# A fourth block evicted by VectorE straight from PSUM, and the weight and key sums moved from GpSimd to VectorE

## The chip, the cores and the metric

The kernel runs on one core of a Trainium2 chip. The metric is the device time of one launch in microseconds (us), lower is better. The core has a matrix engine (TensorE, in the profile PE, with its weight loads as PEld), VectorE (DVE), ScalarE (ACT), GpSimd (POOL), and queues for transfers between HBM and the on-chip memory SBUF, most of them issued by SyncE (SP). Matrix products are written to PSUM banks, from which another engine has to read ("evict") them before the bank is used for something else.

## The reference

One layer of a sequence model over 2048 tokens of width 1024, with 256 context tokens ahead of them. A normalised and modulated input is multiplied by one wide weight matrix `w_in` of 9216 columns. The first 5120 columns belong to eight heads of a gated linear recurrence, which runs over the tokens in both directions and starts from the states that the context leaves; the others to a gated short convolution. Both results, side by side, go through one output matrix.

```python
h  = rmsnorm(x, norm_w) * (1.0 + scale) + shift        # tokens
hc = rmsnorm(ctx, norm_w) * (1.0 + scale_c) + shift_c  # context
p  = h  @ w_in                                         # (2048, 9216)
pc = hc @ w_in[:, :HG_COLS]
...
f = lb + (1.0 - lb) * sigmoid(z)       # forget gates, one set per direction; keys are 1 - f
S_t = diag(f_t) S_{t-1} + k_t v_t^T;  o_t = S_t^T q_t  # both directions
y_hg = head_rmsnorm(o_f + o_b) * silu(gate)
y_cv = bg * conv3(cg * hh, conv_w) * silu(gate_cv)     # columns 5120..9215
x = x + gate_out * (concat([y_hg, y_cv]) @ w_out)
out = rmsnorm(x, final_norm_w)
```

## The kernel before

**Stages.** The profiled execution shows four: the setup (0 to about 235 us: modulation, normalisation and transposition of the tokens, first weights), the heads (to about 1450 us: eight heads, each over four groups of 512 tokens), the convolutions (to about 1985 us: blocks of 128 channels, two groups of tokens at a time) and the output projection.

**Seven products.** Every product of a 2x2 block arrangement is computed by `seven` with seven block products in place of eight, from sums of weight blocks (A11, A12, A22 and S1 to S4) and sums of token blocks (B11, B21, B22 and T1 to T4). Each block product `prod` is done in 16 bits with a high and a low part of both operands, so a block product is three matmuls for each of `nk` slices (lines 839, 840, 841 of the profile). A `seven` unit uses three PSUM banks: `a` (tile `sa`), `b` (`sb`) and `c_` (`sc`). Bank `a` takes A11B11, then S2T2, then S3T3, and last, after the next unit's first product, A22T4 (`finish`); `b` takes S1T1 and then S4B22; `c_` takes A12B21. Between these products values are evicted: `keep` lets ScalarE copy a bank to SBUF with a scale (line 846: p1, p5, u2, u3), and `plus` is one VectorE instruction that reads a bank, scales it and adds a kept tile (line 850). Of the four result blocks, the first and the second are evicted with `plus`; the third is left in bank `a` for a caller's instruction; the fourth (`c22`) is u3 + p5.

**Weights.** `load_pair` brings two blocks of 128 columns of `w_in` into a ring of three stage tiles (`ws_p`), measures their size on ScalarE (line 341) and prepares the left operands in steps that are taken one at a time between products of the unit before: `begin` finds the scale (lines 139 to 147; its last product waits for `rb_p`, line 345) and forms s1 (`s_p`, line 356); `whole` splits A11 and A12 into high (line 151, ScalarE) and low parts (line 152, VectorE), and forms A11 - A21 (line 367); then S1 is split, `sum_a` (line 373) forms S2, A22 and S2 are split, `sum_b` (line 376) forms S4, S3 and S4 are split. The tiles of the low parts are `wloa_p`, `wlob_p` and the lower half of `e_p`. The transfer of a later pair (line 333) waits until a stage tile is no longer read.

**Heads.** A unit gives two blocks of columns for one group: gates `f`, queries `q`, values `vT`, output gates `z`. Keys K and queries Q go through a tree of VectorE products with running decays (lines 414 and 421), and PE needs Q and K at each level (lines 554, 568, 578). `query_end` forms Q from q and f (line 496) and the key sum `ks` of both directions (line 498); `out_gates` multiplies the gate z with its sigmoid (line 713) and stores it.

**What sets the order.** The program is written as lists of steps with weights from a table (`PACE`), which are merged into the products by place; a scheduler then fixes the order of instructions on each engine before launch, and each engine runs its own list strictly in that order, waiting where an operand is not ready. So a moved instruction changes the neighbours of others too.

Of the kernel before, what the change touches and what calls it, by code (L numbers as in the profile page):

```python
# [50 lines left out]
def paced(weight, fn):  # L51
    """A step with its share of the time of its list of steps."""
    return PACE.get(weight, weight), fn
# [7 lines left out]
def hybrid_layer(ctx: ExitStack, tc, x, cx, w_ada, b_ada, w_in, w_out, fnorm_w, small_d, masks, ident_d, sel_d, out):  # L61
# [92 lines left out]
    # ---------------------------------------------------------------- modulation  # L154
# [53 lines left out]
    def norm_group(ntile, src, row0, m, nm, first_ops=None, space=q_tile):  # L208
# [84 lines left out]
        def combine(k, a, b, whole):  # L293
# [13 lines left out]
            if whole:  # L307
                store("B22", k, b22, G, G)
# [9 lines left out]
    # ---------------------------------------------------------------- weights  # L318
# [8 lines left out]
    def load_pair(col0, col1, nm, own=False, a21_at=None):  # L327
        """Two blocks of columns of w_in as left operands of the seven-product scheme."""
# [18 lines left out]
        def begin():  # L347
# [8 lines left out]
            G.tensor_tensor(t["s1"], a21, a22, ALU.add)  # L356
# [8 lines left out]
        def whole():  # L365
            split(w.st, stage[0], t["a"][0], t["a"][1])
            G.tensor_tensor(a21, a11, a21, ALU.subtract)
# [4 lines left out]
        def sum_a():  # L372
            G.tensor_tensor(a11, t["s1"], a11, ALU.subtract)  # L373

        def sum_b():
            G.tensor_tensor(a12, a12, a11, ALU.subtract)
# [5 lines left out]
    # ---------------------------------------------------------------- parameters of the heads  # L382
# [22 lines left out]
    # ---------------------------------------------------------------- recurrent heads  # L405
# [30 lines left out]
    class Seg:  # L436
        """Forget gates, keys, values and queries of one head over one stretch of tokens."""
# [55 lines left out]
        def query_end(s):  # L493
# [4 lines left out]
            G.tensor_tensor(s.ks, s.K[:, :s.n], s.K[:, s.n:], ALU.add)  # L498
# [207 lines left out]
    def out_gates(h1, h2, g, w):  # L706
# [3 lines left out]
        def end(i, h_):  # L710
            r = ring(f"zs{h_.hd}_{g}")
            S.activation(r, z[i], AF.Sigmoid)
            G.tensor_tensor(r, z[i], r, ALU.mult)
# [33 lines left out]
    # ---------------------------------------------------------------- convolution  # L747
    class Conv:
        """One block of channels over the two halves of tokens of one or two groups."""
# [80 lines left out]
    def seven(left, right, nk, n, nm, tick, sx, tmp, done, c11, c12, c21, c22):  # L830
        """Two by two blocks of a product in seven block products."""
# [33 lines left out]
        u3 = keep(a, "u3")  # L865
        c22(lambda dst: G.tensor_tensor(dst, u3, p5, ALU.add))  # L866
# [18 lines left out]
    # ---------------------------------------------------------------- output weights  # L885
# [10 lines left out]
    def load_C(pool, tp, names):  # L896
        """Right operands of the convolutions for the halves of two groups of tokens."""
# [40 lines left out]
    def wo_steps(k):  # L938
        """Operands of the output weights for the seven-product scheme, kept in DRAM."""
# [585 lines left out]
```

## Time and profile before

| what | value |
|---|---|
| time, three runs | 2316.42, 2318.95, 2320.67 us; median 2318.95 us |
| span of the profiled execution | 2317.1 us (its own time is this span; none other is recorded) |
| PE busy | 2140.4 us, 92% of the span |
| PE weight loads | 1478.3 us |
| VectorE busy | 1627.5 us, 70%, 3173 instructions |
| ScalarE busy | 1216.5 us, 53%, 2435 instructions |
| GpSimd busy | 551.4 us, 24%, 549 instructions |
| mean granted TensorE clock | 0.98 in the heads and the convolutions, 0.91 in the setup |

A busy PE is not a PE at full speed: matmuls are pipelined, and in short stretches the granted clock is 0.50. The shares are averages over four stages. Where an instruction is given with an idle time and a releaser, the idle time is that of its engine just before it, and the releaser is what ended the wait.

### The profile page before, as it was taken

To read this page: it belongs to the slowest core of one execution; us is meant where nothing else is said; L and a number is where in the kernel's file an instruction comes from. 1 tells how busy PE (TensorE), PEld (TensorE's weight loads), DVE (VectorE), ACT (ScalarE), POOL (GpSimd) and SP (SyncE) were. 2 spreads that over 40 slices of the span, in tenths; PEclk is the share of its full clock that TensorE was granted. 3 is DMA by queue.
4 is the path that set the end of the run, shared out by engine and by line. 5 is a ranking of instruction groups with operands and counts; after the bars stand their busy time and mean duration, and the time that the engine had idled before them with its cause. 6 is when DMAs were issued, how large, how long until landed. Compare 5 with 4: busy or idle time off the path is not lost.

```text
span 2317.1 us, 52341 instructions
## 1 busy us (share of the span) xinstructions
PE 2140.4 (92%) x21563; PEld 1478.3 (64%) x21563; DVE 1627.5 (70%) x3173; ACT 1216.5 (53%) x2435; POOL 551.4 (24%) x549
## 2 busy tenths in 40 slices
PE   4778799899998999999999999999999999999998
PEld 1667688787886887887878878444344434444443
DVE  6986866777668667777676685586677556677775
ACT  5665656565566565656765754453454333333332
POOL 2433412413124124133241231221122112000001
PEclk8889899999999999999999999999999999999999
DMA  8664333323341343234432538733332132734231
GB/s 308 210 211 166 94 125 100 141 84 106 102 149 68 104 145 105 99 101 147 153 112 91 191 126 276 234 116 105 110 125 102 60 125 74 276 101 145 91 118 55
DMA packets 191044, 309.92 MB, mean 134 GB/s; under 512 B 13138, under 2 KB 123090, under 8 KB 189012
## 3 DMA queue, kind: packets, MB, share of 16 engines
q1 hardware_dynamic: 188644, 302.64, 39.2%
q8 instruction: 169, 2.77, 0.5%
q10 hardware_dynamic: 2160, 3.93, 0.5%
q14 instruction: 71, 0.58, 0.1%
HBM read 241.50 MB, written 65.01 MB: 132 GB/s over the span
## 4 chain that ended last, share of the span: by engine, by line
PE 28%; issue 12%; DVE 6%; ACT 4%; DMA 3%; POOL 1%; SPq 0%; POOLq 0%; ACTq 0%; DVEq 0%
PE sa L839 4%; PE sa L841 4%; PE sa L840 4%; DMA ws_p<-in_w_in 2%; PE sb L839 2%; PE sb L841 2%; PE sb L840 2%; DVE wlob_p L152 1%; DVE e_p L152 1%; PE sc L839 1%; PE sc L840 1%; PE sc L841 1%; PE A L554 1%; DMA wos_a<-in_w_out 1%; ACT whia_p L151 1%
## 5 line engine op out<-in xcount | busy, mean ns | idle before, releaser
L846 ACT ACTIVATE u<-sa,sx_w 128x256 f32<-128x256 f32 (+1 forms) x228 | 118.8, 521 | 180.2 <-PE sa L841 162.9
L840 PEld LDWEIGHTS <-e_p 128*128 128x128 f16 x1368 | 135.3, 99 | 87.9 <-issue 40.0
L414 DVE TENSOR_TENSOR K<-K,tot 128x512 f32<-128x512 f32 x192 | 142.5, 742 | 69.5 <-PE A L578 27.1
L421 DVE TENSOR_TENSOR Q<-Q,tot 128x512 f32<-128x512 f32 x192 | 144.4, 752 | 56.7 <-PE A L554 56.4
L839 PEld LDWEIGHTS <-e_p 128*128 128x128 f16 x1368 | 135.1, 99 | 60.8 <-issue 5.5
L841 PEld LDWEIGHTS <-e_p 128*128 128x128 f16 x1368 | 135.4, 99 | 55.2 <-issue 4.4
L537 ACT ACTIVATE km<-K 128x512 f32<-128x512 f32 x160 | 108.9, 685 | 111.3 <-DVE K L414 81.8
L840 PEld LDWEIGHTS <-whib_p 128*128 128x128 f16 x912 | 90.1, 99 | 51.9 <-issue 17.7
L840 PEld LDWEIGHTS <-whia_p 128*128 128x128 f16 x912 | 89.6, 98 | 44.8 <-issue 13.2
L586 POOL COPY A<-Ac 32x128 f32<-32x128 f32 x128 | 67.3, 525 | 209.6 <-ACT A L582 193.4
L839 PEld LDWEIGHTS <-whib_p 128*128 128x128 f16 x912 | 90.0, 99 | 41.7 <-issue 2.8
L839 PEld LDWEIGHTS <-whia_p 128*128 128x128 f16 x912 | 89.7, 98 | 37.0 <-issue 1.2
L841 PEld LDWEIGHTS <-wlob_p 128*128 128x128 f16 x912 | 90.2, 99 | 35.6 <-issue 0.3
L841 PEld LDWEIGHTS <-wloa_p 128*128 128x128 f16 x912 | 89.6, 98 | 35.8 <-issue 1.6
L151 ACT ACTIVATE e_p<-ws_p,sc_p 128x512 f16<-128x512 f32 x108 | 77.2, 718 | 65.5 <-POOL ws_p L373 33.9
L152 DVE SCALAR_TENSOR_TENSOR e_p<-ws_p,sc_p,e_p 128x512 f16<-128x512 f32 x108 | 107.3, 1032 | 0.2 <-ACT e_p L151 0.2
L373 POOL TENSOR_TENSOR ws_p<-s_p,ws_p 128x512 f32<-128x512 f32 x36 | 56.3, 1564 | 205.2 <-DVE wloa_p L152 175.9
L341 ACT ACTIVATE junk<-ws_p 128x1024 f16<-128x1024 f32 x72 | 75.8, 1053 | 47.9 <-DMA ws_p<-in_w_in 47.6
L554 PE MATMUL A<-Q,km 128*32 128x32 f32 x5120 | 77.5, 203 | 23.9 <-DVE Q L421 21.0
L554 PEld LDWEIGHTS A<-Q,km 128*32 128x32 f32 x5120 | 58.6, 113 | 59.0 <-issue 26.9
L866 POOL TENSOR_TENSOR z<-u,p 128x256 f32<-128x256 f32 (+1 forms) x34 | 35.1, 1034 | 231.7 <-ACT u L846 227.3
L866 POOL TENSOR_TENSOR f<-u,p 128x256 f32<-128x256 f32 x31 | 27.5, 887 | 241.7 <-ACT u L846 241.7
(866 smaller groups left out, 7274.7 us busy)
## 6 DMA issues: line engine op xcount, KB each, us to landing
ws_p<-in_w_in SPq DMA_DIRECT2D x72, 512.0 KB, 4.1
y_o<-yT SPq DMA_DIRECT2D x32, 512.0 KB, 3.7
wa<-in_w_ada SPq DMA_DIRECT2D x16, 512.0 KB, 4.7
Gd<-zs SPq DMA_DIRECT2D x32, 256.0 KB, 3.2
sg<-Gd SPq DMA_DIRECT2D x32, 256.0 KB, 4.0
yT<-y SPq DMA_DIRECT2D x32, 256.0 KB, 2.3
wos_a<-in_w_out SPq DMA_DIRECT2D x16, 512.0 KB, 4.9
yT<-sg SPq DMA_DIRECT2D x64, 128.0 KB, 2.2
```

Of the source, the lines that this page charges most:

```text
L151: S.activation(hi, src, AF.Copy, scale=st[:, 0:1])
L152: V.scalar_tensor_tensor(lo, src, st[:, 0:1], hi, ALU.mult, ALU.subtract)
L341: S.activation(junk.rearrange("p (k n) -> p k n", k=KT), stage[i], AF.Abs, accum_out=r)
L414: V.tensor_tensor(m, m, sub(cur, nb + 1, [[2, np_], [-(nb + 1), 2], [0, B]]), ALU.mult)
L421: V.tensor_tensor(m, m, sub(cur, 1, [[2, np_], [nb - 1, 2], [0, B]]), ALU.mult)
L537: S.activation(sub(s.km, 0, [[2 * B, n // (2 * B)], [B, 2], [1, B]]), mix(s.K, n, B, n // (2 * B)), AF.Copy)
L554: PE.matmul(pt[j * SB:(j + 1) * SB, ch * SB:(ch + 1) * SB], s.km[:, o:o + SB], mix(s.qf, n, B, SB // (2 * B), o), start=True, stop=True)
L586: G.tensor_copy(A3[js, :, js], s.Ac[js])
L839: PE.matmul(ps, hi[:, k], rh, start=start and k == 0, stop=False, skip_group_check=not start)
L840: PE.matmul(ps, hi[:, k], right(name, 1, k), start=False, stop=False, skip_group_check=not start)
L841: PE.matmul(ps, lo[:, k], rh, start=False, stop=k == nk - 1, skip_group_check=not start)
L846: S.activation(r, ps, AF.Copy, scale=sx)
```

## The change

Seven places change engine. In `load_pair` the four weight sums (lines 356, 367, 373, 376) go from GpSimd to VectorE, and so do the key sum (line 498), the product of the output gate (line 713) and the low part of operand B22 in the setup (line 266, called from 308). In `seven`, the fourth block is no longer made of a ScalarE copy u3 and a GpSimd sum u3 + p5; one VectorE instruction reads bank `a`, scales and adds p5. In numbers of instructions: VectorE 342 more (12 + 4x36 + 32 + 32 + 122), ScalarE 122 fewer, GpSimd 554 to 212. The products are the same on PE, and so are the transfers. From line 866 on the changed file is one line shorter.

```diff
@@ combine (token operands)
             if whole:
-                store("B22", k, b22, G, G)
+                store("B22", k, b22, G)
@@ load_pair, begin
-            G.tensor_tensor(t["s1"], a21, a22, ALU.add)
+            V.tensor_tensor(t["s1"], a21, a22, ALU.add)
@@ load_pair, whole
             split(w.st, stage[0], t["a"][0], t["a"][1])
-            G.tensor_tensor(a21, a11, a21, ALU.subtract)
+            V.tensor_tensor(a21, a11, a21, ALU.subtract)
@@ load_pair, sum_a and sum_b
-            G.tensor_tensor(a11, t["s1"], a11, ALU.subtract)
+            V.tensor_tensor(a11, t["s1"], a11, ALU.subtract)
...
-            G.tensor_tensor(a12, a12, a11, ALU.subtract)
+            V.tensor_tensor(a12, a12, a11, ALU.subtract)
@@ Seg.query_end
-            G.tensor_tensor(s.ks, s.K[:, :s.n], s.K[:, s.n:], ALU.add)
+            V.tensor_tensor(s.ks, s.K[:, :s.n], s.K[:, s.n:], ALU.add)
@@ out_gates, end
             S.activation(r, z[i], AF.Sigmoid)
-            G.tensor_tensor(r, z[i], r, ALU.mult)
+            V.tensor_tensor(r, z[i], r, ALU.mult)
@@ seven
         prod(a, "S3", "T3", start=False)
-        u3 = keep(a, "u3")
-        c22(lambda dst: G.tensor_tensor(dst, u3, p5, ALU.add))
+        c22(plus(a, p5))
         prod(b, "S4", "B22", start=False)
         c12(plus(b, u2))
```

The order changes around the moved instructions. The first place is VectorE's list in the heads where the weights of a later unit are prepared while the tree of keys and queries runs (in the profiled execution from 712 us on). Before, the names being `wlob_p` and `e_p` for low parts, `ws_p` and `s_p` for weights in 32 bits, K and Q for the tree, `vT` for a block of values:

```order
L152 SCALAR_TENSOR_TENSOR wlob_p_10160<-s_p_10162,sc_p_10153,whib_p_10159 128x512
L152 SCALAR_TENSOR_TENSOR wlob_p_10160<-ws_p_10093,sc_p_10153,whib_p_10159 128x512
L414 TENSOR_TENSOR K_1_9349<-K_1_9349,tot_1_9866 128x8x2x32
L421 TENSOR_TENSOR Q_1_9843<-Q_1_9843,tot_1_9866 128x8x2x32
L152 SCALAR_TENSOR_TENSOR e_p_10161<-ws_p_10091,sc_p_10153,e_p_10161 128x512
L152 SCALAR_TENSOR_TENSOR e_p_10161<-ws_p_10093,sc_p_10153,e_p_10161 128x512
L152 SCALAR_TENSOR_TENSOR e_p_10161<-ws_p_10091,sc_p_10153,e_p_10161 128x512
L850 SCALAR_TENSOR_TENSOR vT_0_10037<-sb_10097,sx_w_8460,u_52_10170 128x256
```

The same place on VectorE after the change:

```order
L152 SCALAR_TENSOR_TENSOR wlob_p_10088<-s_p_10090,sc_p_10081,whib_p_10087 128x512
L373 TENSOR_TENSOR ws_p_10019<-s_p_10090,ws_p_10019 128x512
L152 SCALAR_TENSOR_TENSOR wlob_p_10088<-ws_p_10021,sc_p_10081,whib_p_10087 128x512
L414 TENSOR_TENSOR K_1_9283<-K_1_9283,tot_1_9796 128x8x2x32
L421 TENSOR_TENSOR Q_1_9773<-Q_1_9773,tot_1_9796 128x8x2x32
L152 SCALAR_TENSOR_TENSOR e_p_10089<-ws_p_10019,sc_p_10081,e_p_10089 128x512
L376 TENSOR_TENSOR ws_p_10019<-ws_p_10019 128x512
L152 SCALAR_TENSOR_TENSOR e_p_10089<-ws_p_10021,sc_p_10081,e_p_10089 128x512
L850 SCALAR_TENSOR_TENSOR q_0_9966<-sa_9967,sx_w_8402,p_52_10040 128x256
L152 SCALAR_TENSOR_TENSOR e_p_10089<-ws_p_10019,sc_p_10081,e_p_10089 128x512
L850 SCALAR_TENSOR_TENSOR vT_0_9965<-sb_10025,sx_w_8402,u_52_10098 128x256
```

Sum L373 now stands ahead of Q, and sum L376 and the eviction of q, the fourth block, stand between Q and vT.

The second place is PE's list at that point, the end of unit 52 and the beginning of unit 53. Before, the tile `sa_52` is bank `a` of unit 52 (its A22T4), `sa_53` that of unit 53, and A5 is a level of the tree that reads Q:

```order
L841 MATMUL sa_53_10251<-hop15B11_9341,wloa_p34_5845 128x256
L839 LDWEIGHTS whib_p11_8008
L839 MATMUL sa_52_10039<-hop15T4_9783,whib_p11_8008 128x256
L840 LDWEIGHTS whib_p11_8008
L840 MATMUL sa_52_10039<-hop15T4_9783,whib_p11_8008 128x256
L841 LDWEIGHTS wlob_p11_8009
L841 MATMUL sa_52_10039<-hop15T4_9783,wlob_p11_8009 128x256
L578 MATMUL A5_3_1_10193<-Q_3_1_9843,K_3_1_9349 64x64 x8
```

The same place on PE after the change:

```order
L841 MATMUL sa_53_10177<-hop15B11_9275,wloa_p34_5809 128x256
L578 MATMUL A5_3_1_10121<-Q_3_1_9773,K_3_1_9283 64x64 x8
L839 LDWEIGHTS e_p34_5812
L839 MATMUL sa_53_10177<-hop15T2_9554,e_p34_5812 128x256
L840 LDWEIGHTS e_p34_5812
L840 MATMUL sa_53_10177<-hop15T2_9554,e_p34_5812 128x256
```

and, at the end of the twelve matmuls of `sa_53` with `e_p34` (S2T2 of unit 53):

```order
L841 LDWEIGHTS e_p34_5812
L841 MATMUL sa_53_10177<-hop15T2_9554,e_p34_5812 128x256
L839 LDWEIGHTS whib_p11_7954
L839 MATMUL sa_52_9967<-hop15T4_9715,whib_p11_7954 128x256
L840 LDWEIGHTS whib_p11_7954
L840 MATMUL sa_52_9967<-hop15T4_9715,whib_p11_7954 128x256
```

A22T4 of unit 52 no longer starts ahead of the product with Q: that product comes first, then the twelve matmuls of S2T2 of unit 53, and A22T4 of unit 52 behind them.

The third place is VectorE's list in a block of the convolutions. Before:

```order
L152 SCALAR_TENSOR_TENSOR wloa_p_22571<-ws_p_22516,sc_p_22566,whia_p_22570 128x1024
L152 SCALAR_TENSOR_TENSOR wlob_p_22573<-s_p_22575,sc_p_22566,whib_p_22572 128x512
L152 SCALAR_TENSOR_TENSOR wlob_p_22573<-ws_p_22518,sc_p_22566,whib_p_22572 128x512
L850 SCALAR_TENSOR_TENSOR b_2_2_22600<-sc_22579,sx_w_22214,p_121_22520 128x512
L152 SCALAR_TENSOR_TENSOR e_p_22574<-ws_p_22516,sc_p_22566,e_p_22574 128x512
L799 TENSOR_TENSOR cv_2_2_22512<-b_2_2_22600,cv_2_2_22512 128x512
L152 SCALAR_TENSOR_TENSOR wpT_2_22612<-wo_2_22389,sc_wo,wpT_2_22612 128x512
L152 SCALAR_TENSOR_TENSOR e_p_22574<-ws_p_22518,sc_p_22566,e_p_22574 128x512
L152 SCALAR_TENSOR_TENSOR e_p_22574<-ws_p_22516,sc_p_22566,e_p_22574 128x512
L826 TENSOR_TENSOR sg_2_2_22630<-z_2_2_22628,sg_2_2_22630 128x512
L850 SCALAR_TENSOR_TENSOR b_2_2_22645<-sb_22522,sx_w_22214,u_121_22577 128x512
```

The same place after the change, `z` being a fourth block there and `b` a second one:

```order
L152 SCALAR_TENSOR_TENSOR wloa_p_22385<-ws_p_22330,sc_p_22380,whia_p_22384 128x1024
L152 SCALAR_TENSOR_TENSOR wlob_p_22387<-s_p_22389,sc_p_22380,whib_p_22386 128x512
L373 TENSOR_TENSOR ws_p_22330<-s_p_22389,ws_p_22330 128x512
L152 SCALAR_TENSOR_TENSOR wlob_p_22387<-ws_p_22332,sc_p_22380,whib_p_22386 128x512
L850 SCALAR_TENSOR_TENSOR b_2_2_22414<-sc_22393,sx_w_22032,p_121_22334 128x512
L152 SCALAR_TENSOR_TENSOR e_p_22388<-ws_p_22330,sc_p_22380,e_p_22388 128x512
L799 TENSOR_TENSOR cv_2_2_22326<-b_2_2_22414,cv_2_2_22326 128x512
L376 TENSOR_TENSOR ws_p_22330<-ws_p_22330 128x512
L152 SCALAR_TENSOR_TENSOR wpT_2_22426<-wo_2_22205,sc_wo,wpT_2_22426 128x512
L152 SCALAR_TENSOR_TENSOR e_p_22388<-ws_p_22332,sc_p_22380,e_p_22388 128x512
L152 SCALAR_TENSOR_TENSOR e_p_22388<-ws_p_22330,sc_p_22380,e_p_22388 128x512
L850 SCALAR_TENSOR_TENSOR z_2_2_22440<-sa_22296,sx_w_22032,p_121_22356 128x512
```

Both sums now stand among the splits, and the eviction of z stands behind the last split, ahead of the eviction of b from `sb`.

## The prediction

> **What bounds the kernel now.** I read the page's busy line first, then the four stages by their windows, then what PE waits for, then single bursts in the timeline. The window columns are busy time of PE, PEld, DVE, ACT and POOL (with counts of instructions), granted clock, share of DMA time, GB/s.
>
> ```profile
> PE 2140.4 (92%) x21563; PEld 1478.3 (64%) x21563; DVE 1627.5 (70%) x3173; ACT 1216.5 (53%) x2435; POOL 551.4 (24%) x549
> ```
>
> ```profile
> 0.00:235.00 235.00, 167.99 (x1824) 124.45 (x1825) 180.76 (x430) 139.13 (x267) 81.52 (x115) 0.91 0.65 221
> 235.00:1450.00 1215.00, 1142.66 (x15912) 981.31 (x15912) 869.62 (x1786) 736.73 (x1651) 332.07 (x341) 0.98 0.38 125
> 1450.00:1985.00 535.00, 508.84 (x2340) 227.32 (x2338) 346.86 (x516) 227.39 (x355) 116.81 (x81) 0.98 0.37 123
> 1985.00:2317.10 332.10, 320.94 (x1489) 145.26 (x1489) 230.23 (x445) 113.29 (x166) 21.01 (x13) 0.99 0.37 121
> ```
>
> PE bounds three of the four stages: it is busy for 94% to 97% of each. So nothing that VectorE, ScalarE or GpSimd do is worth more than what PE is not busy (1215.0 - 1142.7 = 72 us in the heads, 26 in the convolutions, 11 in the output) plus what it loses at a clock below 1.00 (2% of 1215 and of 535 is 24 and 11 us). The time in which PE stands is named by the waits, in us, with their number and the longest:
>
> ```profile
> PE A L554 <- DVE Q L421: 21.0, 15, 4.7
> PE sa L839 <- ACT p L846: 20.5, 10, 3.9
> PE A L578 <- DVE Q L421: 13.4, 7, 2.0
> PE sa L839 <- ACT u L846: 11.5, 10, 5.1
> PE sb L839 <- DVE vT L850: 9.3, 7, 1.7
> ```
>
> Three of the five end on VectorE, at Q and at vT. Seven waits of up to 2.0 and seven of up to 1.7 us point to something that comes once for each turn of the heads. One such turn is this:
>
> ```profile
> 712.18 0.74 DVE L152 SCALAR_TENSOR_TENSOR wlob_p<-s_p,sc_p,whib_p 128x512 f16<-128x512 f32 x1
> 712.41 1.65 POOL L373 TENSOR_TENSOR ws_p<-s_p,ws_p 128x512 f32<-128x512 f32 x1 [7.87 <-DVE wloa_p L152]
> 712.85 1.76 DVE L152 SCALAR_TENSOR_TENSOR wlob_p<-ws_p,sc_p,whib_p 128x512 f16<-128x512 f32 x1
> 714.13 1.59 POOL L376 TENSOR_TENSOR ws_p<-ws_p 128x512 f32<-128x512 f32 x1
> 714.52 1.75 DVE L414 TENSOR_TENSOR K<-K,tot 128x512 f32<-128x512 f32 x1
> ...
> 714.94 0.27 PE L839 MATMUL sa<-hop15T,whib_p 128*128 128x256 f16 x1
> ...
> 715.69 1.17 POOL L866 TENSOR_TENSOR q<-u,p 128x256 f32<-128x256 f32 x1
> 716.20 1.21 DVE L421 TENSOR_TENSOR Q<-Q,tot 128x512 f32<-128x512 f32 x1
> 716.82 1.72 POOL L498 TENSOR_TENSOR ks<-K 128x512 f32<-128x512 f32 x1
> 717.33 3.15 DVE L152 SCALAR_TENSOR_TENSOR e_p<-ws_p,sc_p,e_p 128x512 f16<-128x512 f32 x3
> 717.46 0.69 PE L578 MATMUL A<-Q,K 128*64 128x64 f32 x16 [2.03 <-DVE Q L421]
> ...
> 720.40 0.47 DVE L850 SCALAR_TENSOR_TENSOR vT<-sb,sx_w,u 128x256 f32<-128x256 f32 x1
> 720.79 0.71 DVE L414 TENSOR_TENSOR K<-K,tot 128x512 f32<-128x512 f32 x1
> 720.93 0.27 PE L839 MATMUL sb<-hop15T,whib_p 128*128 128x256 f16 x1 [1.69 <-DVE vT L850]
> 721.42 0.68 DVE L421 TENSOR_TENSOR Q<-Q,tot 128x512 f32<-128x512 f32 x1
> ```
>
> VectorE works without a gap from 712.18 to 721, and PE stands for 2.03 us at Q and for 1.69 at vT. The same instruction has two durations here: the low part `wlob_p` took 0.74 when it had begun before L373, and 1.76 when L373 had begun before it; K 1.75 behind the start of L376 and 0.71 with no GpSimd sum beside it; Q 1.21 and 0.68. What makes VectorE late is the GpSimd work beside it, which costs it about 1.0 us for each sum of 128x512.
>
> **The change part by part.** Prices come from these rows (busy time, mean ns of one, idle time ahead):
>
> ```profile
> L373 POOL TENSOR_TENSOR ws_p<-s_p,ws_p 128x512 f32<-128x512 f32 x36 | 56.3, 1564 | 205.2 <-DVE wloa_p L152 175.9 <-issue 22.8 <-PE sc L841 6.3
> L498 POOL TENSOR_TENSOR ks<-K 128x512 f32<-128x512 f32 x32 | 45.5, 1421 | 0.0
> L1426 DVE TENSOR_TENSOR x_o<-x_o,r_o 128x512 f32<-128x512 f32 x32 | 22.0, 687 | 0.4
> L850 DVE SCALAR_TENSOR_TENSOR f<-sb,sx_w,u 128x256 f32<-128x256 f32 x31 | 14.8, 478 | 18.7 <-PE sb L841 18.7
> L846 ACT ACTIVATE u<-sa,sx_w 128x256 f32<-128x256 f32 (+1 forms) x228 | 118.8, 521 | 180.2 <-PE sa L841 162.9
> ```
>
> *Added work.* A 128x512 sum on VectorE with no GpSimd beside it takes 0.69 us (L1426), an eviction of 128x256 with a sum 0.48 (L850; by the burst's rows about 0.74 for 512 columns would be the price of any such pass). 4x36 weight sums, 32 key sums and 32 gate products make 208 x 0.69 = 143 us; the 122 evictions at 0.48 to 0.74 are 59 to 90, taken as 70 since most are of 256 columns; the 12 low parts 12 x 0.48 = 6. VectorE gets about 219 us more.
>
> *Removed work.* ScalarE loses 122 x 0.52 = 64 us, GpSimd 342 instructions of 0.9 to 1.6 us. ScalarE's share is worth little, since the waits that end on ScalarE are put down to p and the other u, which stay; p is taken up below. For VectorE, the rows of the burst give 1.02 lost by `wlob_p`, 1.04 by K, 0.53 by Q and 3.15 - (3 x 0.74 - 0.14) = 1.07 by the three `e_p` (0.07 being what neighbours overlap): 3.7 us beside four moved instructions, 0.9 each. At 330 instructions, of which perhaps half run while VectorE has work (its 70%), that is 150 us. VectorE would stand some 70 us higher, at 73%, and no closer to being the bound; what counts is where in the bursts it is late.
>
> *The burst of the heads, in the order after.* The list is now wlob, L373, wlob, K, Q: 0.74 + 0.69 + 0.74 + 0.71 + 0.68 - 4 x 0.07 = 3.28, so Q ends at 715.46 in place of 717.41, and the wait of 2.03 at L578 shrinks to about 0.1. Then e, L376, e, q, e, vT: 3 x 0.74 + 0.69 + 2 x 0.47 - 5 x 0.07 = 3.50, and vT ends at 718.96, not 720.87. Ahead of A22T4 PE now has L578 (0.69) and S2T2, twelve matmuls that start 0.11 us after each other, 1.3 us. It would reach A22T4 at 717.5, where before it began at 714.94 with bank `a` long free. The bank is now freed by q on VectorE, at 715.46 + 0.74 + 0.69 + 0.74 + 0.47 - 4 x 0.07 = 717.8: 0.3 us late. A22T4 lasts until 719.1, when vT is done. PE begins the product behind vT at 719.1, against 720.93, and has S2T2 behind it, another 1.3: a gain of 3.1 against 3.72 stood. I take 2.7 for each of the seven, since the work behind may wait elsewhere: **-19 us** (between 0 and -22.7, the two rows of waits).
>
> *The waits at L554.* These come in the third burst of a turn:
>
> ```profile
> 751.75 0.65 PE L554 MATMUL A<-Q,km 128*32 128x32 f32 x32 [2.34 <-DVE Q L421]
> ...
> 744.00:751.00 7.00, 4.31 (x64) 3.29 (x63) 6.94 (x10) 4.43 (x7) 5.11 (x4) 0.99 0.38 115
> 751.00:757.80 6.80, 6.05 (x87) 4.27 (x88) 5.51 (x10) 5.01 (x8) 1.27 (x2) 0.50 0.41 144
> ```
>
> VectorE is busy 6.94 of 7.00 us there and GpSimd 5.11. After, Q stands ahead of the splits, but other levels stand behind them. I take a third of the 21.0: **-7 us** (0 to -21).
>
> *Late fourth blocks.* Every A22T4 now waits for VectorE in place of ScalarE. Away from the bursts VectorE has idle time and a 0.48 eviction is done as a 0.52 copy was; nothing. In the bursts the eviction stands behind splits. There are three bursts a turn, 24 in all; seven have the gain above, 0.3 late being in it. For the other 17 I take 0.3 each: **+5 us** (0 to +49: at worst 717.8 - 714.94 = 2.9 us each, if PE has nothing to do ahead of it).
>
> *Key sum, gate product.* Both are VectorE work of 0.69 behind the instructions that PE waits for (ks behind Q's first product, the gate product before a store). The two gate products stand on VectorE right behind z and wait for a sigmoid on ScalarE; what is queued behind them is a later Q. 32 of 0.69 with 0.5 of waiting would be +16 if PE waited for each; I take 0, since PE has a unit's products ahead of that Q; the work that covers it is those products, and where they are gone it costs the 0.69.
>
> *The convolutions.* PE waits for p, which stands behind a size measurement on ScalarE, which waits for a transfer:
>
> ```profile
> 1630.98 1.76 DVE L152 SCALAR_TENSOR_TENSOR wlob_p<-s_p,sc_p,whib_p 128x512 f16<-128x512 f32 x1
> 1632.67 1.75 DVE L152 SCALAR_TENSOR_TENSOR wlob_p<-ws_p,sc_p,whib_p 128x512 f16<-128x512 f32 x1
> ...
> 1635.00 3.07 DVE L152 SCALAR_TENSOR_TENSOR e_p<-ws_p,sc_p,e_p 128x512 f16<-128x512 f32 x3
> ...
> 1639.37 0.56 SPq L333 DMA_DIRECT2D ws_p<-in_w_in  x1
> ...
> 1644.55 1.06 ACT L341 ACTIVATE junk<-ws_p 128x1024 f16<-128x1024 f32 x1 [1.49 <-DMA ws_p<-in_w_in]
> ...
> 1646.93 0.58 PE L839 MATMUL sa<-C0T,e_p 128*128 128x512 f16 x1 [3.87 <-ACT p L846]
> ```
>
> The transfer's tile is freed when the splits end, at 1638.1. After the change the two `wlob_p` and three `e_p` lose 1.02 + 1.01 + 0.99 = 3.0 us, and L373, L376 and the z or u eviction add 0.69 + 0.69 + 0.74 - 0.21 = 1.9: the transfer is issued 1.1 us earlier, if SP's list has nothing of its own ahead. With half of it in the other kind of block, 0.8 us for each of eight, of the 2.6 that 20.5 / 8 makes: **-6 us** (+8 to -20: above nothing, if the eviction of z ahead of b holds PE by 0.9 a block).
>
> *Clock.* The two windows above show 0.50 in a stretch in which PE was busy 6.05 of 6.80, behind one in which it stood for 2.7 of 7.00. The clock costs at most 24 + 11 us in the two stages; if a sixth of these stretches goes with the waits, **-5 us** (0 to -35). [...]
>
> *Setup and output.* In the setup VectorE is busy 180.76 of 235.00, about as much as PE; its 12 low parts and first weight sums add what the slowing takes off: 0 (-8 to +8, 12 of 0.7 either way). In the output GpSimd has 21.0 us and PE 320.94 of 332.10: 0. The low part's cover is ScalarE's next operand, and if that is gone it costs 0.48 each, which is in the 8.
>
> Sum: -19 - 7 + 5 - 6 - 5 = -32. From the span 2317.1 that is 2285; the median of the three runs stands 1.85 above the span, so I forecast **2286 us**.
>
> **The rivals.**
>
> *A, slower: the fourth block's eviction holds PE.* ScalarE did the u3 copy at once (idle ahead of it at `sa` L841 162.9 us, so it is an engine that waits for PE); VectorE in a burst is busy 6.94 of 7.00. If in the 17 other bursts A22T4 has nothing ahead of it, each loses up to 2.9, +49 and not +5, and the third of L554 is lost too: -19 + 49 - 6 + 0 = +24, **2343 us**. It decides when the average lateness in those 17 passes 1.5 us (17 x 1.5 = 25, the gain of the first burst and of the convolutions). For it: the q eviction stands behind L376 and two splits. Against it: in the burst PE's list has S2T2 ahead of A22T4.
>
> *B, the same: nothing is won in the bursts.* The added 0.69 eats up the 0.9 of slowing removed, PE's waits go from Q and vT to the next thing, and the convolutions stay at the transfer (1.49 us of waiting at L341). Then only the +5 and a few us of clock stand: **2316 to 2321 us**. Against it: in the burst four moved instructions give 3.7 and cost 0.69 x 2 + 0.47, because ks comes later. [...]
>
> *C, more: the clock stays up.* If most waits in the bursts go below what takes the clock to 0.50, 24 of the 35 us come on top of -32: **2261 us**. The window 744 to 751 shows that it takes only 2.7 us of standing, so that most would have to vanish.
>
> *D: VectorE is slow in the bursts for another reason* (ScalarE's splits, transfers); then the moved sums are only added: 7 x (0.69 + 1.85) + 8 x 1.9 = +33, **2352 us**. Against it: K and Q took 0.71 and 0.68 at 720.79 and 721.42, in the same burst.
>
> **How the numbers follow.** Main case 0.54 (its own range 2270 to 2304), C 0.12, B 0.14, A 0.16, D 0.04. The range reaches from C to a mild A: 2258 to 2332, leaving out about half of A and D and the ends of C, 0.18. Runs of this kernel lie 0.2% apart (2316.42 to 2320.67), so 0.2%, 4.6 us, is what can be told from no change. Faster: the main case, C and 0.03 of B, 0.69; same: 0.09 of B and 0.02 of A, 0.11; slower: 0.14 of A, D and 0.02 of B, 0.20.
>
> **What would show it.** Right: VectorE's `wlob_p` and `e_p` at 0.74 all through the bursts; L578's wait for Q below 3 us in all; vT's wait below 4; VectorE busy near 1700 us; p's wait in the convolutions below 15. Wrong: waits of `sa` L839 for a fourth block on L850 (f, q, z, v) above 20 us in all; splits still at 1.7; a clock of 0.50 in more stretches than now.

## The result, and the profile after

The changed kernel took 2224.82 us (median; 2221.22 to 2226.32) against 2317.68 us for the kernel before on the same chip: a ratio of 0.9598, with a 95% interval of 0.9583 to 0.9613. That is 93 us less, where I had forecast 32 less; the way was right and the size was almost three times mine, and the time lies below my range. The profiled execution has a span of 2222.2 us, 94.9 below the one before.

The page's busy line after:

```profile
PE 2113.2 (95%) x21563; PEld 1466.6 (66%) x21563; DVE 1659.9 (75%) x3515; ACT 1158.3 (52%) x2313; POOL 112.5 (5%) x207
```

GpSimd fell from 551 to 113 us, and VectorE rose by 32 us only, though it took over 342 instructions for which I had counted 219 us. PE was busy for 27 us less with the same 21563 matmuls.

The stages have to be cut at the same work, not at the same time, since everything comes earlier. These are the windows of the kernel before, cut at the first low part of the heads' second pair of weights, at the convolutions' first product and at the output's first product (columns as in the prediction):

```profile
0.00:246.30 246.30, 179.11 (x1943) 133.09 (x1944) 191.66 (x456) 146.49 (x282) 84.36 (x120) 0.90 0.64 218
246.30:1459.80 1213.50, 1139.31 (x15865) 979.51 (x15864) 867.61 (x1777) 735.63 (x1645) 333.06 (x338) 0.98 0.37 124
1459.80:2014.00 554.20, 529.08 (x2398) 233.11 (x2398) 357.40 (x523) 232.26 (x358) 116.03 (x81) 0.98 0.39 130
2014.00:2317.10 303.10, 292.93 (x1360) 132.62 (x1358) 210.79 (x420) 102.17 (x152) 17.95 (x11) 0.99 0.35 112
```

And of the kernel after, cut at the same places:

```profile
0.00:236.40 236.40, 178.38 (x1942) 134.21 (x1943) 188.82 (x496) 143.03 (x276) 43.69 (x83) 0.91 0.68 227
236.40:1382.50 1146.10, 1120.71 (x15864) 968.39 (x15862) 887.76 (x1989) 700.28 (x1564) 64.64 (x122) 1.00 0.40 131
1382.50:1919.00 536.50, 521.15 (x2402) 231.34 (x2402) 367.58 (x606) 216.22 (x331) 0.00 (x0) 1.00 0.41 134
1919.00:2222.20 303.20, 292.92 (x1360) 132.62 (x1358) 215.72 (x427) 98.79 (x143) 4.16 (x3) 0.99 0.34 112
```

Each stage's loss of time splits into two: the time that PE was not busy (length less PE's busy time), and the busy time itself, which for the same matmuls moves with the clock.

| stage | length | PE not busy | PE busy (clock) |
|---|---|---|---|
| setup | -9.9 | 67.2 to 58.0: -9.2 | -0.7 |
| heads | -67.4 | 74.2 to 25.4: -48.8 | -18.6 |
| convolutions | -17.7 | 25.1 to 15.4: -9.8 | -7.9 |
| output | +0.1 | +0.1 | 0.0 |

So about 68 us are waits of PE, and 27 us are the clock, whose mean went from 0.98 to 1.00 in the heads and the convolutions. That the busy time follows the clock can be worked out: in stretches at a clock of 0.50, PE was busy for 40.9 us of the heads before and for 3.4 after, and for 18.7 us of the convolutions before and for none after. Half of the differences is 18.8 and 9.3 us, near the 18.6 and 7.9 of the table.

What PE waited for in the heads, before (the same stretch as in the windows; us in total, times, longest):

```profile
PE A L554 <- DVE Q L421: 13.7, 12, 2.5
PE A L578 <- DVE Q L421: 13.4, 7, 2.0
PE sa L839 <- ACT u L846: 11.2, 9, 5.1
PE sb L839 <- DVE vT L850: 9.3, 7, 1.7
PE ss_p L139 <- DVE rb_p L345: 6.8, 5, 1.8
```

and after:

```profile
PE sa L839 <- ACT u L846: 3.1, 2, 2.9
PE A L554 <- DVE Q L421: 3.1, 5, 1.4
...
PE sa L839 <- DVE q L850: 1.7, 7, 0.3
PE A L578 <- DVE Q L421: 1.7, 5, 0.3
PE u L1332 <- DVE f L850: 1.4, 1, 1.4
PE ss_p L139 <- DVE rb_p L345: 1.3, 3, 0.6
```

The wait for vT is gone from the list, all the others have shrunk to a third or less, and 4.5 us of waits at line 740 are new. Of the fourth blocks only q (1.7 us) and z (0.2, further down the list) hold PE in the heads; the `f` of line 850 in this list is a first block, which VectorE reads from bank `c_`. The burst of the prediction, in the timeline after:

```profile
676.85 0.74 DVE L152 SCALAR_TENSOR_TENSOR wlob_p<-s_p,sc_p,whib_p 128x512 f16<-128x512 f32 x1
677.51 0.68 DVE L373 TENSOR_TENSOR ws_p<-s_p,ws_p 128x512 f32<-128x512 f32 x1
678.12 0.74 DVE L152 SCALAR_TENSOR_TENSOR wlob_p<-ws_p,sc_p,whib_p 128x512 f16<-128x512 f32 x1
678.78 0.68 DVE L414 TENSOR_TENSOR K<-K,tot 128x512 f32<-128x512 f32 x1
679.38 0.68 DVE L421 TENSOR_TENSOR Q<-Q,tot 128x512 f32<-128x512 f32 x1
...
680.12 0.69 PE L578 MATMUL A<-Q,K 128*64 128x64 f32 x16 [0.35 <-DVE Q L421]
680.65 0.68 DVE L376 TENSOR_TENSOR ws_p<-ws_p 128x512 f32<-128x512 f32 x1
...
681.91 0.47 DVE L850 SCALAR_TENSOR_TENSOR q<-sa,sx_w,p 128x256 f32<-128x256 f32 x1
...
682.44 0.27 PE L839 MATMUL sa<-hop15T,whib_p 128*128 128x256 f16 x1 [0.22 <-DVE q L850]
...
682.97 0.47 DVE L850 SCALAR_TENSOR_TENSOR vT<-sb,sx_w,u 128x256 f32<-128x256 f32 x1
...
683.74 0.27 PE L839 MATMUL sb<-hop15T,whib_p 128*128 128x256 f16 x1
```

Every VectorE instruction here has, within 0.03 us, the duration that I had taken from rows without GpSimd beside them.

### The profile page after: what moved, and what is told of

Its sections match the earlier page's. It is cut to its first block, busy times and chain, and to the rows that moved or that the text cites. A ratio compares the mean times of both kernels' runs of the same rounds, so it can differ in the third digit from the quotient of the medians.

```text
span 2222.2 us, 51962 instructions
## 1 busy us (share of the span) xinstructions
PE 2113.2 (95%) x21563; PEld 1466.6 (66%) x21563; DVE 1659.9 (75%) x3515; ACT 1158.3 (52%) x2313; POOL 112.5 (5%) x207
## 4 chain that ended last, share of the span: by engine, by line
PE 66%; DVE 15%; DMA 7%; ACT 6%; issue 4%; SPq 1%; POOL 1%; POOLq 0%; DVEq 0%; ACTq 0%
PE sa L839 8%; PE sa L841 7%; PE sa L840 7%; PE sb L839 4%; PE sb L840 3%; PE sb L841 3%; DMA ws_p<-in_w_in 3%; PE sa_o L839 2%; PE sa_o L841 2%; PE sa_o L840 2%; PE A L554 2%; PE T L602 2%; PE sc L839 2%; PE sc L841 2%; PE sc L840 2%
## 5 line engine op out<-in xcount | busy, mean ns | idle before, releaser
L414 DVE TENSOR_TENSOR K<-K,tot 128x512 f32<-128x512 f32 x192 | 132.0, 688 | 61.8 <-PE A L578 24.6
L421 DVE TENSOR_TENSOR Q<-Q,tot 128x512 f32<-128x512 f32 x192 | 132.6, 691 | 33.3 <-PE A L554 32.9
L846 ACT ACTIVATE u<-sa,sx_w 128x256 f32<-128x256 f32 (+1 forms) x114 | 59.8, 524 | 70.9 <-PE sa L841 56.1
L554 PE MATMUL A<-Q,km 128*32 128x32 f32 x5120 | 77.9, 202 | 12.4 <-DVE Q L421 6.4
L554 PEld LDWEIGHTS A<-Q,km 128*32 128x32 f32 x5120 | 58.9, 112 | 46.4 <-issue 20.3
L762 ACT ACTIVATE cv<-c,small 128x512 f32<-128x512 f32 (+1 forms) x36 | 24.2, 671 | 109.2 <-DVE c L780 48.9
L152 DVE SCALAR_TENSOR_TENSOR e_p<-ws_p,sc_p,e_p 128x512 f16<-128x512 f32 x108 | 78.0, 743 | 2.5 <-ACT e_p L151 2.4
L846 ACT ACTIVATE p<-sb,sx_w 128x256 f32<-128x256 f32 (+1 forms) x114 | 59.3, 520 | 35.6 <-PE sb L841 34.0
L846 ACT ACTIVATE p<-sa,sx_w 128x256 f32<-128x256 f32 (+1 forms) x114 | 58.8, 516 | 32.2 <-PE sa L841 32.1
```

Source lines behind the costliest of these rows:

```text
L152: V.scalar_tensor_tensor(lo, src, st[:, 0:1], hi, ALU.mult, ALU.subtract)
L414: V.tensor_tensor(m, m, sub(cur, nb + 1, [[2, np_], [-(nb + 1), 2], [0, B]]), ALU.mult)
L421: V.tensor_tensor(m, m, sub(cur, 1, [[2, np_], [nb - 1, 2], [0, B]]), ALU.mult)
L554: PE.matmul(pt[j * SB:(j + 1) * SB, ch * SB:(ch + 1) * SB], s.km[:, o:o + SB], mix(s.qf, n, B, SB // (2 * B), o), start=True, stop=True)
L846: S.activation(r, ps, AF.Copy, scale=sx)
```

## The experiments

My theory was theory 1: a GpSimd sum beside a VectorE instruction with operands in SBUF makes VectorE late (in the prediction's burst 1.76 us for a split of 0.74), and PE waits for VectorE at the turns of the heads. The rivals were theory 2 (the sums are themselves on the path of the weights, and last half as long on VectorE) and theory 3 (ScalarE is relieved of 122 copies).

### Each part of the change alone

Only the weight sums (before, with):

```diff
-            G.tensor_tensor(t["s1"], a21, a22, ALU.add)
+            V.tensor_tensor(t["s1"], a21, a22, ALU.add)
...
-            G.tensor_tensor(a21, a11, a21, ALU.subtract)
+            V.tensor_tensor(a21, a11, a21, ALU.subtract)
...
-            G.tensor_tensor(a11, t["s1"], a11, ALU.subtract)
+            V.tensor_tensor(a11, t["s1"], a11, ALU.subtract)
...
-            G.tensor_tensor(a12, a12, a11, ALU.subtract)
+            V.tensor_tensor(a12, a12, a11, ALU.subtract)
```

> The kernel before, with only the four weight sums (lines 356, 367, 373, 376) moved to VectorE. Theory 1, GpSimd work beside VectorE slows VectorE: the time goes down in the share that these sums have in VectorE's lost time (about 100 of 152 us by comparing its instructions with and without GpSimd beside them), so about -60 us of the -93 of the whole change (2250 to 2268). Theory 2, the sums are on the path of the preparation and last 1.5 us on GpSimd and 0.7 on VectorE: nearly all of it, -80 to -93. Theory 3, ScalarE is relieved by the 122 copies that go: at most -40.

Only the fourth block:

```diff
-        u3 = keep(a, "u3")
-        c22(lambda dst: G.tensor_tensor(dst, u3, p5, ALU.add))
+        c22(plus(a, p5))
```

> The kernel before, with only the fourth block evicted by VectorE from PSUM (no ScalarE copy, no GpSimd sum). Theory 1: about -17 us (25 of 152 us of VectorE's lost time), less what late evictions cost. Theory 2: 0, between -5 and +10. Theory 3, 64 us of ScalarE copies no longer stand ahead of p, u and the size measurement for which PE waits: -40 or more.

Only key sum, gate product and B22 part:

```diff
-            G.tensor_tensor(s.ks, s.K[:, :s.n], s.K[:, s.n:], ALU.add)
+            V.tensor_tensor(s.ks, s.K[:, :s.n], s.K[:, s.n:], ALU.add)
...
-            G.tensor_tensor(r, z[i], r, ALU.mult)
+            V.tensor_tensor(r, z[i], r, ALU.mult)
...
-                store("B22", k, b22, G, G)
+                store("B22", k, b22, G)
```

> The kernel before, with only the key sum, the gate product and the low part of B22 moved to VectorE. Theory 1: about -14 us (some 25 of 152 us of lost time). Theories 2 and 3: 0, between -5 and +10, since none of the three is on the path of the weights or on ScalarE.

Measured against 2318.28 us before on the same chip: the sums 2277.30 (41 less; ratio 0.9840, 0.9809 to 0.9871), the fourth block 2316.01 (2 less; 0.9992, 0.9976 to 1.0007, not told from nothing), the key sum and the rest 2303.56 (15 less; 0.9949, 0.9930 to 0.9969). These are differences of medians; by the ratios the three are 37, 2 and 12 us, so a part's size is good to some 4 us. Theory 2's number for the sums (-80 to -93) was missed by half. Theory 3's bound for the sums (at most -40) was about met, but its number for the fourth block (-40) was missed altogether. Theory 1 had the key sum right (-14) and overrated the other two (-60, -17). And the three parts make 58 us, not 93.

The busy line of the kernel with the sums alone moved speaks for theory 1:

```profile
PE 2123.5 (94%) x21563; PEld 1470.5 (65%) x21563; DVE 1620.5 (71%) x3317; ACT 1214.6 (53%) x2435; POOL 346.6 (15%) x405
```

VectorE ran 144 instructions more than before and was busy for 7 us less (1627.5 before). At the 0.68 us that such a sum takes on VectorE, the moved sums are 98 us, so its other instructions took about 105 us less. The waits of the kernel before speak against theory 2: in the heads and the convolutions no row of PE or of its weight loads waits for a weight sum or for a split of weights (lines 151 and 152), so there the length of the sums held PE up only through other work.

For the key sum a second cause is open, which none of the theories had. In the kernel before, VectorE itself stood for it:

```profile
DVE K L414 <- POOL ks L498: 43.9, 18, 3.3
```

This wait goes with the move too, and the runs do not divide the 15 us between it and the slowing.

### Each part taken back

> The kernel after, with the four weight sums back on GpSimd (so only the fourth block, key sum, gate product and B22 part are on VectorE). The parts alone gave -41 (sums), -2 (fourth block) and -15 us (key sum and the rest) of -93; 35 us belong to parts together. If the parts add up but for one pair that contains the sums: 2301 (-17 from before). If the fourth block and the key sum help each other without the sums: 2270 to 2285.

> The kernel after, with the fourth block again made by a ScalarE copy and a GpSimd sum (so sums, key sum, gate product on VectorE). Theory I1, the fourth block on VectorE pays only where the splits ahead of it are short, that is with the sums off GpSimd: the time is then that of the two other parts added up, 2262 (-56), between 2255 and 2268. Theory I2, the missing 35 us lie between the sums and the key sum (whichever GpSimd work is left comes to lie beside the splits): 2225 to 2235.

> The kernel after, with key sum, gate product and B22 part back on GpSimd (so sums and fourth block on VectorE). Theory I1: 2240 (the whole change less the 15 us of this part, -78), between 2235 and 2248. Theory I2: 2275 (-43), between 2268 and 2280.

The edits are the diffs above, taken back in the kernel after. Against 2318.50 us: without the sums 2287.82 (0.9870, 0.9844 to 0.9897), without the fourth block 2250.94 (0.9709, 0.9685 to 0.9732), without the key sum and the rest 2250.28 (0.9698, 0.9667 to 0.9730). The run without the sums fell between its two cases (2301, and 2270 to 2285). With these, all combinations of the three parts are measured:

| moved | us less than before | the parts added up |
|---|---|---|
| sums | 41 | |
| fourth block | 2 | |
| key sum, gate product, B22 part | 15 | |
| sums and fourth block | 68 | 43 |
| sums and key sum etc. | 68 | 56 |
| fourth block and key sum etc. | 31 | 17 |
| all | 93 | 58 |

Neither I1 (35 us between sums and fourth block alone) nor I2 (between sums and key sum) stands: every pair gives 12 to 25 us more than its parts (16 to 31 by the ratios). The fourth block shows a part of why. Moved alone, it brings VectorE's eviction into bursts that the GpSimd sums still draw out; this is what PE then waited for:

```profile
PE A L554 <- DVE Q L421: 23.1, 19, 3.8
PE A L578 <- DVE Q L421: 20.3, 8, 2.9
PE sa L839 <- DVE z L850: 14.0, 18, 1.6
```

The wait for Q at L578 rose from 13.4 to 20.3. Of the 14.0 us for z, 7.5 are for the fourth block (from bank `a`) and 6.4 for a first block (from bank `c_`), which had 1.8 before. In the heads (cut as in the windows above) PE was not busy for 80.4 us, against 74.2 before, while the convolutions became 8 us shorter. So in the heads this is my slower rival (the fourth block's eviction holds PE), in a small size and only with everything else left on GpSimd: with the key sum and its group moved and the sums still on GpSimd, the fourth block was worth 16 us (31 - 15), and with the sums moved 27 us (68 - 41).

Most of that worth lies in the convolutions. They took 557.0 us with the fourth block back on ScalarE and GpSimd, 546.3 with the sums back on GpSimd, and 536.5 in the kernel after.

### What the fourth block gains from

> The kernel after, with the fourth block made by a ScalarE copy of bank a (as before) and the sum with p5 on VectorE from SBUF. Nothing of it is on GpSimd, VectorE has the same number of instructions, ScalarE 122 more, and bank a is freed by ScalarE. If the cause of the gain is that GpSimd is silent: 2220 to 2232, the same as after, or up to 10 us less if the waits for fourth blocks (about 12 us in after) were the price of VectorE's eviction. If ScalarE's relief is a part of the gain: 2240 or more.

```diff
-        c22(plus(a, p5))
+        u3 = keep(a, "u3")
+        c22(lambda dst: V.tensor_tensor(dst, u3, p5, ALU.add))
```

Measured: 2238.42 us (0.9651, 0.9627 to 0.9674), 13 us more than after and 13 less than with GpSimd's sum (2250.94). It fell between the two numbers. So the 26 us that the fourth block is worth, with the rest moved, fall into two halves. One goes when the sum moves from GpSimd to VectorE, where it is also shorter (a sum of 128x512 takes 0.68 us on VectorE in after; the fourth block's of that size took 1.46 on GpSimd in the kernel before, as a mean), the other when ScalarE's copy goes. The second half can be theory 3, but need not be: with the copy in the way VectorE stood for it for 58.9 us (its rows for z, u, q and f, 18.1, 14.2, 13.4 and 13.2 us), and the order on PE is another in each of the three kernels. The runs do not divide this. A wait for VectorE's evictions was no price worth saving; in after the waits for fourth blocks come to 9.1 us, not 12.

### GpSimd work that nobody waits for

This is the run that shows theory 1 by itself. Two GpSimd sums for each pair of weights were put into the kernel after; their results are never read, and the order on PE, VectorE and ScalarE is the same as in after.

```diff
             V.tensor_tensor(a11, t["s1"], a11, ALU.subtract)
+            G.tensor_tensor(t["s1"], a11, a11, ALU.add)
...
             V.tensor_tensor(a12, a12, a11, ALU.subtract)
+            G.tensor_tensor(t["s1"], a12, a12, ALU.add)
```

> The kernel after, with two more GpSimd sums of 128x512 for each pair of weight blocks, one right behind each of the sums of lines 373 and 376, into a tile that nothing reads any more; 72 in all, and the order of instructions on PE, VectorE and ScalarE is the same as after. Nothing waits for their values. Theory 1: each costs VectorE 0.5 to 1.0 us where it is busiest, so +25 to +45 us. Theories 2 and 3: 0 to +5.

The control has the same two instructions, two columns wide (`t["s1"][:, :1, :2]` and so on):

> The control of the run with two idle GpSimd sums for each pair of weights: the same two instructions at the same places, with the same life of the tile that they write, but two columns wide. The order on PE, VectorE and ScalarE is that of after. If the 35 us that those sums cost come from GpSimd's time beside VectorE: 2220 to 2232, as after. If they come from the tile's longer life or from two more waits: 2245 or more.

And the same sums three times each:

> The kernel after with each of those two idle GpSimd sums done three times (216 in all, the same order on PE, VectorE and ScalarE). If GpSimd's time beside VectorE sets the loss: three times the dose gives 2.0 to 3 times the 35 us, 2295 to 2330, and the granted clock falls to 0.50 again in those stretches of the heads that follow a stretch of 3.4 us in which PE was busy for less than about 0.45. If the loss was a fixed one for each place: 2255 to 2265.

Measured: 2259.34 us with the sums (0.9760, 0.9739 to 0.9781), 34.5 us more than after; 2227.66 with the control (0.9615, 0.9599 to 0.9631), as after; 2352.39 with three times the sums (1.0150, 1.0135 to 1.0165), 128 us more than after and slower than the kernel before. The sums and the control came out as theory 1 expected. Three times the sums cost 3.7 times as much as the first dose, above the 2295 to 2330 that I expected.

Between the first dose and the control only the length of the GpSimd sums differs (behind line 373, 0.84 us as a mean with two columns and 1.71 with all). Of waits for them there is one of 0.4 us in the first dose, on ScalarE, and none in the control, so the 34.5 us are GpSimd's time beside VectorE. The triple dose is not as clean: there the transfer of later weights did wait for the idle sums, which read the tile that it fills:

```profile
SPq L333 <- POOL s_p L382: 44.1, 23, 3.4
```

What this added to the 128 us is not known.

The group of the splits into `e_p`, which run beside these sums, shows what VectorE loses (busy time, mean ns). Before, after, with the sums, and with three times the sums:

```profile
L152 DVE SCALAR_TENSOR_TENSOR e_p<-ws_p,sc_p,e_p 128x512 f16<-128x512 f32 x108 | 107.3, 1032 | 0.2 <-ACT e_p L151 0.2
```

```profile
L152 DVE SCALAR_TENSOR_TENSOR e_p<-ws_p,sc_p,e_p 128x512 f16<-128x512 f32 x108 | 78.0, 743 | 2.5 <-ACT e_p L151 2.4
```

```profile
L152 DVE SCALAR_TENSOR_TENSOR e_p<-ws_p,sc_p,e_p 128x512 f16<-128x512 f32 x108 | 107.8, 1018 | 2.1 <-ACT e_p L151 2.1
```

```profile
L152 DVE SCALAR_TENSOR_TENSOR e_p<-ws_p,sc_p,e_p 128x512 f16<-128x512 f32 x108 | 141.8, 1333 | 2.3 <-ACT e_p L151 2.3
```

The page's busy lines with the sums and with three times the sums:

```profile
PE 2114.7 (94%) x21563; PEld 1465.4 (65%) x21563; DVE 1696.0 (75%) x3515; ACT 1159.1 (51%) x2313; POOL 224.3 (10%) x279
```

```profile
PE 2149.0 (91%) x21563; PEld 1478.6 (63%) x21563; DVE 1786.5 (76%) x3515; ACT 1159.4 (49%) x2313; POOL 425.3 (18%) x423
```

VectorE ran the same 3515 instructions in 36.1 and 126.6 us more than after, and the span grew by 31.3 (to 2253.5) and 128.8 (to 2351.0). So the time that VectorE loses here is time of the kernel, nearly one for one. The second line also holds the clock: at the first dose PE's busy time rose by 1.5 us, at the triple dose by 35.8, at a mean granted clock of 0.970. The fourth blocks appear too; with three times the sums PE waited (line numbers are shifted by the added lines):

```profile
PE sa L845 <- DVE z L856: 36.2, 15, 3.8
...
PE sa L845 <- DVE q L856: 19.1, 8, 2.7
PE sa L845 <- DVE u L856: 18.5, 4, 4.6
```

where after has 2.2 us for z, 1.7 for q and 5.2 for u. A split of 0.74 us lasted up to 1.79 beside a sum in the kernel before. There, 87 of the 180 splits into `wlob_p` and `e_p`, whose operands are all in SBUF, took more than 0.9 us, each of them beside a GpSimd instruction; the 33 that had none beside them all took less. VectorE's evictions there, which read a PSUM bank (line 850, 128x256), took 0.47 us as a mean in the 34 cases with GpSimd beside them for at least half of their time, and 0.48 in the 132 with none.

### What is left on GpSimd

> The kernel after, with the 72 casts of token operands (line 263), most of what is left on GpSimd in the setup, given to ScalarE. If GpSimd beside VectorE still costs some 10 us in the setup: 2212 to 2220. If ScalarE's time in the setup is dearer: 2225 to 2235.

```diff
-                G.tensor_scalar(hi, src, 1.0, 0.0, ALU.mult, ALU.add)
+                S.activation(hi, src, AF.Copy)
```

Measured: 2220.75 us (0.9580, 0.9566 to 0.9595). The interval overlaps that of after (0.9583 to 0.9613), so a gain of some 4 us is likely and not shown. The time lies just outside the first range. It is the fastest of the kernels here.

## Why the prediction was right in its way and wrong in its size

The terms of the sum, measured in us of the profiled span with the stages cut as above:

| term | forecast | measured |
|---|---|---|
| heads, the waits at L578 and for vT | -19 | -19.3 |
| heads, the waits at L554 | -7 | -10.6 |
| heads, late fourth blocks elsewhere | +5 | +0.2 |
| heads, `sa` for u and the size product for `rb_p` | 0 | -13.6 |
| heads, all other waits | 0 | -5.5 |
| convolutions, waits | -6 | -9.8 |
| clock, heads and convolutions | -5 | -26.5 |
| setup | 0 | -9.9 |
| output | 0 | +0.1 |
| sum | -32 | -94.9 |

The mechanism was right: every wait that I had expected to shrink did. What failed is the size of the clock's term, and that the waits named ScalarE or `rb_p`, and the setup, were put at nothing. (2285 and 1.85 make 2287; I wrote 2286.)

**The burst of the heads was right.** From the start of `wlob_p` I had 3.28 us to the end of Q, 5.6 to the freeing of bank `a`, 6.78 to the end of vT, and PE at the product behind it after 6.9. The timeline after has 3.21 (676.85 to 680.06), 5.5 (682.38), 6.59 (683.44) and 6.89 (683.74); the lateness of q's eviction, 0.3 forecast, is 0.22. The term of -19 us, for L578 and vT, measured: 13.4 + 9.3 = 22.7 became 1.7, and 1.7 for q came new: -19.3.

**The late fourth blocks were overrated in the heads**: +5 forecast for the bursts other than the seven, 0.2 measured (z); the 1.7 of q stands in those seven. In the convolutions u and z are fourth blocks too, and I had put their cost only into the range; over the whole span after they come to

```profile
PE sa L839 <- DVE u L850: 5.2, 4, 1.3
...
PE sa L839 <- DVE z L850: 2.2, 6, 0.5
```

That this cost can grow where VectorE is slowed is shown by the triple dose above, with 73.8 us for z, q and u.

**The clock was the term most wrongly sized**: -5 forecast, -26.5 measured (-18.6 and -7.9 of PE's busy time). I took a sixth of the half-speed stretches to go with the waits; nearly all of them went (from 240 to 2000 us, 68.3 us of them before and 3.4 after). With all 35 us that they cost at most, my sum would have been -62. These windows of the kernel before show why. In the traces of before and after all 30 stretches at 0.50 begin on a grid of 3.41 us, so I cut the windows there:

```profile
716.79:720.20 3.41, 1.77 (x25) 1.45 (x26) 3.41 (x4) 1.12 (x3) 3.01 (x5) 1.00 0.00 0
747.52:750.93 3.41, 1.20 (x10) 0.68 (x7) 3.41 (x4) 1.52 (x3) 3.03 (x2) 1.00 0.27 77
750.93:754.34 3.41, 2.60 (x42) 1.97 (x43) 3.41 (x6) 2.56 (x5) 1.34 (x2) 0.50 0.00 0
```

In the first window PE was busy for 1.77 us of 3.41 (0.52), and the clock stayed at 1.00 behind it. In the second it was busy for 1.20 (0.35), and the window behind it has 0.50. In the traces of before and after, 1006 such windows from 240 to 2000 us are at full clock. In 14 of them PE was busy for less than 0.41 of the window, and the next one was at 0.50 each time; in 988 it was busy for more than 0.48, and the next one never was; of the four between (0.412, 0.419, 0.468, 0.473) it was behind 0.419 and 0.473. So in these two traces the stretches at 0.50 go with the sum of the waits in the window ahead of them, and not with the length of one wait. In the kernel before, PE stood for 2.03 us of one window (1351.67 to 1355.08) in two waits of at most 1.49, and the clock went down; a single wait of 3.36 us (up to 1507.28), with 2.01 in one window and the rest in the one ahead of it, did not take it down. Of the fifteen windows of the kernel before that had a stretch at 0.50 behind them, seven were within 0.28 us of a busy share of 0.48, and the others within 0.95; after has one such window. With the sums alone moved, PE's busy time was already down to 2123.5 us from 2140.4. Rival C (the clock stays up), to which I had given 0.12, is what happened to the clock.

**The other waits of the heads were left out.** L554 was put at -7, as a third of 21.0 us over the whole span, and gave -10.6 in the heads (13.7 to 3.1) and 4 more in the setup (21.0 to 6.4 over the whole). I had given nothing to the wait of `sa` for ScalarE's u (11.2 to 3.1) and to that of the size product for `rb_p` (6.8 to 1.3): 13.6 us more. The five rows that I had listed were not PE's five longest: the 10.5 us for `rb_p` over the whole span stand above vT's 9.3 and were not among them. And I had said that the waits put down to ScalarE stay. But u has its place on ScalarE's list behind instructions that themselves wait for VectorE or for the bursts' splits. Two places of the kernel before, in the timeline:

```profile
254.82 0.42 ACT L265 ACTIVATE hpT_x<-ha_x 128x256 f16<-128x256 f32 x1 [2.39 <-DVE ha_x L305]
255.15 0.46 ACT L846 ACTIVATE u<-sa,sx_w 128x256 f32<-128x256 f32 x1
255.66 0.37 PE L839 MATMUL sa<-hop3T,e_p 128*128 128x256 f16 x1 [5.06 <-ACT u L846]
...
747.25 0.71 ACT L151 ACTIVATE e_p<-ws_p,sc_p 128x512 f16<-128x512 f32 x1
747.87 0.45 ACT L846 ACTIVATE u<-sa,sx_w 128x256 f32<-128x256 f32 x1
748.37 0.27 PE L839 MATMUL sa<-hop15T,whib_p 128*128 128x256 f16 x1 [0.69 <-ACT u L846]
```

In the first, u follows a cast that waited 2.39 us for a VectorE instruction (line 305, 1.48 us beside a GpSimd sum), and PE stood for 5.06; in the second it follows a split. So the row that named ScalarE was in part a wait for the same late VectorE. For `rb_p` I have only the smaller total, not a traced reason.

**The convolutions** were put at -6; -9.8 of waits and -7.9 of clock came. The row of p went from 20.5 to

```profile
PE sa L839 <- ACT p L846: 5.3, 6, 2.9
```

over the whole span. Moving the sums alone left the convolutions at 553.4 us and the fourth block alone brought them to 546.2 (cut as in the windows above), so here the fourth block had to move before the splits, on which I built the term, could count. With the sums alone moved, the wait for p in the convolutions fell by 8.0 us (20.5 to 12.5), not far from my 6, but a wait of 12.6 us for c (line 784) that I had not seen came in its place. The fourth block alone eased p as much (to 13.7) and brought no such wait; with both moved, p is at 4.1, c at 2.7, and the fourth blocks u and z cost 7.0.

**The setup** (cut as above) was put at 0 (-8 to +8) and gave -9.9, outside that range. The sums alone gave -4.5 of it, the key sum's group, which holds the B22 parts, -3.6. I had set the added work equal to the slowing that goes; VectorE's busy time there fell from 191.66 to 188.82 us with 40 instructions more.

**VectorE's total** was to rise by 70 us and rose by 32.4: with the 219 us of added work, the slowing that went was about 187 us and not 150.

**Rival B** (nothing is won in the bursts) failed on a price: in the burst a sum on GpSimd cost VectorE about 1.0 us, and on VectorE it takes 0.68. L373 took 1.56 us on GpSimd as a mean. That a move between engines that hinder each other pays because the work is shorter on the other one fits these rows; it was not tested by itself.

What stays open: why the pairs exceed their parts by just these amounts. That the bursts' waits hide one another, and that in before and after, from 240 to 2000 us, the clock went to 0.50 only behind windows with PE busy for 0.17 to 0.47 of them, both make for it, and the runs do not divide it between the two; the clock was not varied by itself. Open are also the shares of copy and sum in the fourth block's worth, and of the key sum's two causes.

## What to carry to other kernels

If the same instruction shows two durations, look for what runs beside it: here GpSimd sums of 1.5 us, off every chain, cost the kernel nearly what they cost VectorE (31.3 us of the span for 36.1 of VectorE's busy time), and the kernel with VectorE at 75% and GpSimd nearly silent is faster than the one with VectorE at 70% and GpSimd's help. Cut a change's effect on the matrix engine into waits and clock, and where the clock falls to half, sum up all the standing time ahead of it (in the 16 cases above 1.80 to 2.83 us of 3.41); where a small saving keeps the clock up, it can be worth several times its size (an estimate from the rows above: 0.28 us less standing, for a stretch at 0.50 that costs up to half of 3.41 us). Parts of such a change should not be judged one at a time: a move worth nothing alone was worth 26 us with the others.

## What the runs showed of the hardware that I had not expected

In the traces of before and after, each of the 14 windows of 3.41 us in which the matrix engine was busy for less than 0.41 of it was followed by one at a granted clock of 0.50, even where no single wait was longer than 1.5 us (1351.67 to 1355.08 in the kernel before), and none of the 988 above 0.48 was (both from 240 to 2000 us). And GpSimd sums stretched a VectorE split of 128x512 from 0.74 to as much as 1.79 us in the kernel before, while two GpSimd sums of two columns each, in the places where the full ones cost 34.5 us, cost nothing that could be measured (2227.66 against 2224.82 us).
